# The up product of an MLP by seven products of halves, with its result sent through DRAM and the down product behind it

## The chip, the core and the metric

The kernel runs on one core of a Trainium2 chip. The time is that of one execution on the device, in microseconds. Of the core's engines five matter: TensorE (PE, with its weight loads as PEld), VectorE (DVE), ScalarE (ACT), GpSimd (POOL) and SyncE (SP), which here only issues DMAs. Each works off its own instructions in a fixed order and waits for the others by semaphores.

## What is computed

One decoder layer for 512 tokens of width 2048: an RMSNorm, three kinds of mixing heads, an output projection with residual, a second RMSNorm, and an MLP with the square of a ReLU; at the end one more RMSNorm. All is float32. The change is in the last third:

```python
    x = x + y @ w_out
    h2 = rmsnorm(x, norm2_w)
    return x + jnp.square(jax.nn.relu(h2 @ w_up)) @ w_down
...
    return rmsnorm(x, final_norm_w)
```

`w_up` is 2048 x 8192, `w_down` 8192 x 2048.

## The kernel before

**Numbers in halves.** Every float32 factor is split into a high part of type float32r (a cast on ScalarE) and a low part (the source minus the high part, on VectorE). `mm3` (lines 106 to 110) then makes a product of three matmuls: high by high, high by low, low by high. A weight tile that comes in by DMA costs one cast and one subtraction (`wload`, lines 96 to 104, for 128 x 512; `split`, lines 806 to 808, for 128 x 1024).

**Output projection** (lines 738 to 758). For each of 16 blocks m of 128 features 48 matmuls of 512 columns give the new x, feature by row. ScalarE and VectorE split it, scaled by the norm's weight, into `xw2[m]`; POOL adds up its squares; `turn` transposes it for the residual `xq`, which stays in SBUF token by row.

**Up product** (`up_chunk`, lines 765 to 777). For each of 64 blocks f of 128 hidden features four weight chunks of 256 KB are loaded and split, and 48 matmuls with `xw2` as the 512 moving columns give h. VectorE applies ReLU and the norm's factor `Rb`, ScalarE squares into `hp`.

**Down product** (`unit`, lines 881 to 912). Blocks of four f are multiplied with 1024 x 512 weights by seven products of halves in place of eight (Strassen's way in Winograd's form): h is cut in two by tokens and by features, the weights by features and by outputs. `a_prep` makes the seven left sides, four of them sums of h, `w_prep` the seven right sides from four quarters of 512 KB (`quarter`), four of them by a subtraction in place on VectorE or two. Each of the seven units has 12 matmuls of 512 columns, and VectorE adds its result to one or two of the four parts of `xq` (line 877).

**Order.** Up and down stand interleaved: `up_chunk` for block b + 1 before each unit of block b, so that a unit is followed by 12 matmuls that don't depend on it. The last block of four is multiplied plainly (`last`, line 944) and followed by the final norm. A scheduler places the other engines' instructions; weight loads have a raised priority (`DPRIO`, `APRIO`). All DMAs are issued by SP. PSUM tiles and SBUF pools are cyclic: a tile waits until the one that had its place is read.

Of the kernel before, what the change touches and what calls it, by code (L numbers as in the profile page):

```python
# [11 lines left out]
F32 = mybir.dt.float32  # L12
# [4 lines left out]
P = 128  # L17
# [11 lines left out]
FBLK = 4  # L29
ORDER = [10, 11, 12, 6, 7, 8, 9, 0, 1, 2, 3, 13, 4, 14, 5, 15]  # L30
# [23 lines left out]
def trunk(ctx, tc, xT, wv1, wv2, wa, wo, wu, wd, vec, wf, out, dbg=None):  # L54
# [655 lines left out]
    ps_l = psum_pool("ps_l", r=1, t=2)  # L710
# [7 lines left out]
    late = ctx.enter_context(tc.tile_pool(name="late", bufs=1, reuse_waits="tile"))  # L718

    xq = [[[late.tile([P, 2, 512], F32, name=f"xq{h}{d}{j}") for j in range(2)] for d in range(2)] for h in range(2)]  # L720

    def xw2t(shape, name, dt):
        return late.tile(shape, dt, name=name, tag="xw2", bufs=16, align_bytes=256)

    x1, xw2 = [], []
    acc2 = big_pool.tile([P, 512], F32, name="acc2", tag="acc")

    def turn(m):

        d, j = divmod(m // 4, 2)  # L730
        for q in range(m % 4, m % 4 + 2):
            p = xps("t")
            for b in range(NB):
                PE.transpose(p[:, b * P:(b + 1) * P], x1[m - m % 4 + q][:, b * P:(b + 1) * P], ident)  # L734
            for h in range(2):
                S.copy(out=xq[h][d][j][:, :, q * P:(q + 1) * P],
                       in_=p[:, h * 256:h * 256 + 256].rearrange("p (i f) -> p i f", i=2))

    for m in range(KT):
        xr = big_pool.tile([P, 512], F32, name="xr", tag="xr", bufs=6)  # L740
        nc.sync.dma_start(out=xr, in_=xT[:, m, :])
        p = gemm(wo[m], yh)
        x = big_pool.tile([P, 512], F32, name="x1", tag="xr", bufs=6)
        V.tensor_tensor(out=x, in0=p, in1=xr, op=ALU.add)
        a = xw2t([P, 2, 512], "xw2", F32R)
        w = col(C_N2 + m)
        S.activation(out=a[:, 0], in_=x, func=AF.Copy, scale=w)
        V.scalar_tensor_tensor(out=a[:, 1], in0=x, scalar=w, in1=a[:, 0].bitcast(F32),
                               op0=ALU.mult, op1=ALU.subtract)
        if m == 0:  # L750
            S.activation(out=acc2, in_=x, func=AF.Square)
        else:
            sq = tmp()
            S.activation(out=sq, in_=x, func=AF.Square)
            G.tensor_tensor(out=acc2, in0=acc2, in1=sq, op=ALU.add)
        x1.append(x)
        xw2.append(a)
        if m % 2 == 0 and m:
            turn(m - 2)

    nblk = FF // P // FBLK
    HK = FBLK // 2
    hp = {}

    def up_chunk(f, c, st):

        if c == 0:
            st["p"] = mmps()
        p = st["p"]
        gemm_chunk(p, wu[f], xw2, c)  # L770
        if c == KT // CHUNK_KT - 1:
            g = f // HK
            if f % HK == 0:
                hp[g] = late.tile([P, HK, 512], F32, name="hp", tag="hp", bufs=3)
            t = tmp()
            V.scalar_tensor_tensor(out=t, in0=p, scalar=0.0, in1=Rb, op0=ALU.max, op1=ALU.mult)
            S.activation(out=hp[g][:, f % HK], in_=t, func=AF.Square)


    ust = {}  # L780
    NCH = KT // CHUNK_KT
    Rb = per.tile([P, 512], F32, name="Rb")
    for n in range(FBLK * NCH):
        if n == 1:
            p = xps("r")
            PE.matmul(p, lhsT=ones, rhs=acc2, start=True, stop=True)
            rsqrt_exp(Rb, p, 1.0 / D, None)
        if n == 2:
            turn(KT - 2)
        up_chunk(n // NCH, n % NCH, ust)  # L790
    ps_l.__exit__(None, None, None)
# [3 lines left out]


    mlp = ctx.enter_context(tc.tile_pool(name="mlp", bufs=1, reuse_waits="tile", side="right"))
    psd = tc.tile_pool(name="ps_m", bufs=1, space=bass.MemoryType.PSUM, reuse_waits="tile")
    psd_pool = psd.__enter__()
    pool_of_mm[:] = [psd_pool, 2]  # L800
    PROD = (1, 2, 5, 6, 3, 7, 4)

    def pair(role):
        return psd_pool.tile([P, 2, 512], F32, name="pp", tag=f"pp{role}", bufs=1)
# [4 lines left out]

    AC = {}  # L810
    HT = T // 2

    def atile(n):
        return mlp.tile([P, 2, HK, HT], F32R, name=f"A{n}", tag=f"A{n}", bufs=1, align_bytes=256)

    def a_prep(b, n):

        h0, h1 = hp[2 * b], hp[2 * b + 1]
        A11, A21, A12, A22 = h0[:, :, :HT], h0[:, :, HT:], h1[:, :, :HT], h1[:, :, HT:]
        sub = lambda o, x, y: V.tensor_tensor(out=o, in0=x, in1=y, op=ALU.subtract)  # L820

        def sums(m):
            AC[b, "s", m] = t = mlp.tile([P, HK, HT], F32, name="s", tag="s", bufs=2)
            return t

        with tc.high_priority(APRIO):
            if n == 5:
                V.tensor_tensor(out=sums(5), in0=A21, in1=A22, op=ALU.add)
            elif n == 6:
                sub(sums(6), AC[b, "s", 5], A11)  # L830
            elif n == 3:
                sub(sums(3), A12, AC[b, "s", 6])
            elif n == 7:
                sub(sums(7), A11, A21)
            AC[b, n] = o = atile(n)
            split(o, {1: A11, 2: A12, 4: A22}[n] if n in (1, 2, 4) else AC[b, "s", n])

    def quarter(b, j, kh, d):
        q = mlp.tile([P, HK, 512], F32, name="q", tag="q", bufs=5)
        nc.sync.dma_start(out=q, in_=wd[b, j, kh, d])  # L840
        return q

    def w_tile():
        return mlp.tile([P, 2, HK, 512], F32R, name="W", tag="W", bufs=3, align_bytes=256)

    def w_prep(b, j, n, st):

        with tc.high_priority(DPRIO):
            sub = lambda o, x, y: V.tensor_tensor(out=o, in0=x, in1=y, op=ALU.subtract)
            if n == 1:  # L850
                st["11"] = quarter(b, j, 0, 0)
                st["21"] = quarter(b, j, 1, 0)
                st["12"] = quarter(b, j, 0, 1)
                src = st["11"]
            elif n == 2:
                st["22"] = quarter(b, j, 1, 1)
                src = st["21"]
            elif n == 5:
                sub(st["11"], st["12"], st["11"])
                sub(st["12"], st["22"], st["12"])  # L860
                src = st["11"]
            elif n == 6:
                sub(st["11"], st["22"], st["11"])
                src = st["11"]
            elif n == 3:
                src = st["22"]
            elif n == 7:
                src = st["12"]
            else:
                sub(st["21"], st["21"], st["11"])  # L870
                src = st["21"]
            o = w_tile()
            split(o, src)
        return o
# [156 lines left out]
```

## Time and profile before

| | |
|---|---|
| median of three runs | 2233.23 us (2233.19 to 2234.73) |
| the profiled execution | 2231.28 us |
| its span in the profile | 2229.5 us |
| mean granted TensorE clock | 0.997 |
| matmuls recorded | 10394 |
| DMA traffic | 227.07 MB, mean 102 GB/s |

A page of the profile gives each engine's busy time and its share of the span, then the chain of work that ended last. Groups of instructions read: line, engine, operation, output tile <- input tiles, shape, count, then the busy time of the group, the mean of one in ns, and the idle time of the engine just before them with what ended it. Matmuls overlap each other in a pipe, so their pace is seen from the starts of two that follow each other, not from their durations. Windows give the busy time and the number of instructions of each engine in a stretch of the span.

### The profile page before, as it was taken

The page shows a single profiled execution, that of the slowest core. Times are in us where ns is not written, and L with a number is a line of the kernel's source. Part 1 is how long each engine was busy: PE and PEld are TensorE (multiplying, and loading weights), DVE is VectorE, ACT ScalarE, POOL GpSimd, SP SyncE. Part 2 cuts the span into 40 slices and gives each one's busy share as a digit, 9 for nine tenths or more (in the row PEclk, how much of TensorE's full clock was granted, in tenths as well). Part 3 has the DMA queues.
Part 4 walks back from the last instruction along what each step waited for, and adds up shares of the span by engine and source line. Part 5 has one row for each costly group of instructions (what it writes and reads, how often), then busy time and mean ns, then how long its engine had stood idle before and what let it go on. Part 6 is the DMA issues. An engine that isn't in the chain of part 4 may idle for free.

```text
span 2229.5 us, 28060 instructions
## 1 busy us (share of the span) xinstructions
PE 2202.9 (99%) x10394; PEld 1829.7 (82%) x10394; DVE 1610.3 (72%) x2269; ACT 947.5 (42%) x1571; POOL 69.0 (3%) x111
## 2 busy tenths in 40 slices
PE   9999999999999999999999999999999999999998
PEld 8887787778988888888888888888888888888886
DVE  6689899844666533477777777878878878778774
ACT  5745565333445433433334333333333434333434
POOL 0000000000000011000000000000000000000003
PEclk9999999999999999999999999999999999999999
DMA  6332223233222344433333333333343333333332
GB/s 188 99 98 85 71 82 87 80 90 85 81 84 82 108 114 118 144 107 109 95 110 112 87 110 107 92 117 100 94 123 91 101 112 92 111 104 95 116 111 80
DMA packets 112506, 227.07 MB, mean 102 GB/s; under 512 B 18448, under 2 KB 20624, under 8 KB 112368
## 3 DMA queue, kind: packets, MB, share of 16 engines
q1 hardware_dynamic: 112368, 225.26, 34.2%
q8 instruction: 82, 1.34, 0.3%
q14 instruction: 56, 0.46, 0.1%
HBM read 218.53 MB, written 6.68 MB: 101 GB/s over the span
## 4 chain that ended last, share of the span: by engine, by line
PE 90%; DVE 6%; DMA 1%; issue 1%; ACT 1%; SPq 0%; ACTq 0%; DVEq 0%
PE mm L108 19%; PE mm L109 19%; PE mm L110 19%; PE pp L110 9%; PE pp L109 9%; PE pp L108 9%; DVE wlo L103 1%; DVE Yq L437 1%; DVE tq L435 1%; PE mm L273 1%; PE mm L271 1%; PE mm L272 1%; DVE cv L341 1%; DMA raw<-in_wa_dram 0%; PE t L734 0%
## 5 line engine op out<-in xcount | busy, mean ns | idle before, releaser
L102 ACT CAST whi<-raw 128x512 fp32r<-128x512 f32 (+1 forms) x544 | 333.2, 613 | 613.8 <-PE mm L109 556.2
L103 DVE TENSOR_TENSOR wlo<-raw,whi 128x512 fp32r<-128x512 f32 (+1 forms) x544 | 371.4, 684 | 240.0 <-ACT whi L102 227.9
L877 DVE TENSOR_TENSOR xq<-pp,xq 128x1024 f32<-128x1024 f32 x240 | 290.8, 1222 | 203.1 <-PE pp L110 200.6
L108 PE MATMUL mm<-big,whi 128*128 128x512 f32 x1024 | 404.2, 395 | 2.2 <-DVE tmp L556 1.6
L110 PE MATMUL mm<-big,wlo 128*128 128x512 f32 x1024 | 403.3, 394 | 0.0
L109 PE MATMUL mm<-big,whi 128*128 128x512 f32 x1024 | 403.1, 394 | 0.0
L108 PE MATMUL mm<-xw,whi 128*128 128x512 f32 x1024 | 398.8, 389 | 0.0
L110 PE MATMUL mm<-xw,wlo 128*128 128x512 f32 x1024 | 398.4, 389 | 0.0
L109 PE MATMUL mm<-xw,whi 128*128 128x512 f32 x1024 | 398.3, 389 | 0.0
L807 ACT CAST W<-q 128x1024 fp32r<-128x1024 f32 x210 | 220.8, 1051 | 401.4 <-PE pp L110 398.7
L108 PE MATMUL pp<-W,A 128*128 128x512 f32 x840 | 326.8, 389 | 0.0
L109 PE MATMUL pp<-W,A 128*128 128x512 f32 x840 | 326.8, 389 | 0.0
L110 PE MATMUL pp<-W,A 128*128 128x512 f32 x840 | 326.8, 389 | 0.0
L808 DVE TENSOR_TENSOR W<-q,W 128x1024 fp32r<-128x1024 f32 x210 | 255.5, 1217 | 1.7 <-ACT W L807 1.7
L108 PEld LDWEIGHTS mm<-big,whi 128*128 128x128 f32 x1024 | 192.6, 188 | 41.2 <-DVE tmp L556 1.8
L109 PEld LDWEIGHTS mm<-xw,whi 128*128 128x128 f32 x1024 | 192.4, 188 | 40.2 <-issue 0.2
L110 PEld LDWEIGHTS mm<-big,wlo 128*128 128x128 f32 x1024 | 192.6, 188 | 39.7 <-DVE wlo L103 0.6
L108 PEld LDWEIGHTS mm<-xw,whi 128*128 128x128 f32 x1024 | 192.1, 188 | 40.1 <-issue 0.2
L110 PEld LDWEIGHTS mm<-xw,wlo 128*128 128x128 f32 x1024 | 192.0, 188 | 39.8
L109 PEld LDWEIGHTS mm<-big,whi 128*128 128x128 f32 x1024 | 192.7, 188 | 38.7 <-DVE big L715 0.3
L110 PEld LDWEIGHTS pp<-W,A 128*128 128x128 f32 x840 | 157.8, 188 | 32.9
L108 PEld LDWEIGHTS pp<-W,A 128*128 128x128 f32 x840 | 157.7, 188 | 32.7
(263 smaller groups left out, 2099.2 us busy)
## 6 DMA issues: line engine op xcount, KB each, us to landing
raw<-in_wu_dram SPq DMA_DIRECT2D x256, 256.0 KB
q<-in_wd_dram SPq DMA_DIRECT2D x128, 512.0 KB
raw<-in_wa_dram SPq DMA_DIRECT2D x192, 256.0 KB
raw<-in_wo_dram SPq DMA_DIRECT2D x64, 256.0 KB
xr<-in_xT_dram SPq DMA_DIRECT2D x32, 256.0 KB
raw<-in_wv_dram SPq DMA_DIRECT2D x16, 256.0 KB
out_dram<-xq SPq DMA_DIRECT2D x16, 256.0 KB
raw<-in_wv_dram SPq DMA_DIRECT2D x16, 134.0 KB
```

The source lines that it names most:

```text
L102: S.copy(out=hi[:, :n], in_=raw[:, :n])
L103: V.tensor_tensor(out=lo[:, :n], in0=raw[:, :n], in1=hi[:, :n].bitcast(F32), op=ALU.subtract)
L108: PE.matmul(p, lhsT=lh, rhs=rh, start=first, stop=False, skip_group_check=more)
L109: PE.matmul(p, lhsT=lh, rhs=rl, start=False, stop=False, skip_group_check=more)
L110: PE.matmul(p, lhsT=ll, rhs=rh, start=False, stop=last, skip_group_check=more)
L271: PE.matmul(o, lhsT=xw[k][:, 0, s], rhs=hi[:, ws], start=k == 0 and b % 2 == 0, stop=False)
L272: PE.matmul(o, lhsT=xw[k][:, 0, s], rhs=lo[:, ws], start=False, stop=False)
L273: PE.matmul(o, lhsT=xw[k][:, 1, s], rhs=hi[:, ws], start=False, stop=k == KT - 1 and b % 2 == 1)
L341: V.scalar_tensor_tensor(out=cv, in0=xp[:, i:i + 512], scalar=w(i), in1=cv, op0=ALU.mult, op1=ALU.add)
L807: S.copy(out=o[:, 0], in_=src)
L808: V.tensor_tensor(out=o[:, 1], in0=src, in1=o[:, 0].bitcast(F32), op=ALU.subtract)
L877: V.tensor_tensor(out=x, in0=p, in1=x, op=ALU.add)
```

## The change

The up product is now done by seven products of halves too, for two blocks f at a time (`up_pair`, 32 of them). The left sides are weights: a pair's 2048 x 256 weights lie in DRAM as four quarters of 128 x 1024 (by parity of the input block and by f); the right sides are halves of x by tokens and by parity of the input block, and their sums, which are made and split during the output projection (`XP`, `XS`, and x22 through DRAM). A product has 8 x 3 matmuls of 256 columns.

The weight sums are made differently, for up and down alike (`w_prep`): three quarters t, v and u are loaded by SP; t grows by the fourth quarter through a DMA that accumulates (issued by POOL, for product 5), by u on VectorE (6) and by v on VectorE (4); u grows by the fourth quarter through a second accumulating DMA (7). The order of products is 1, 2, 5, 6, 3, 4, 7. Signs move to the sums of x and of h.

Each pair's h and its four sums go to DRAM in one store of 1 MB (`hs`). After all of up the down product runs alone, in 8 blocks of eight f (the last one with four, and four by the plain product): its left sides are read back from `hs` and split (`a_prep`), each unit has 24 matmuls with two weight tiles, and the residual is read back from DRAM (`xs`).

```diff
-    PROD = (1, 2, 5, 6, 3, 7, 4)
+    PROD = (1, 2, 5, 6, 3, 4, 7)
...
+    def w_prep(n, st, src):
+
+        with tc.high_priority(DPRIO):
+            more = lambda t, kh, d: nc.gpsimd.dma_start(out=t, in_=src(kh, d), accum_op=ALU.add)
+            more_on_v = lambda t, u: V.tensor_tensor(out=t, in0=t, in1=u, op=ALU.add)
+            if n == 1:
+                st["t"] = quarter(src(0, 0))
+                st["v"] = quarter(src(1, 0))
+                st["u"] = quarter(src(1, 1))
+            elif n == 5:
+                more(st["t"], 0, 1)
+            elif n == 6:
+                more_on_v(st["t"], st["u"])
+            elif n == 4:
+                more_on_v(st["t"], st["v"])
+            elif n == 7:
+                more(st["u"], 0, 1)
+            o = mlp.tile([P, 2, 1024], F32R, name="W", tag="W", bufs=3, align_bytes=256)
+            split(o, st[{2: "v", 3: "u", 7: "u"}.get(n, "t")])
+        return o
...
+    def up_pair(g):
...
+        def mms(n, lo, hi):
+            p = banks[n]
+            for i in range(lo, hi):
+                xh, xl = x_side(n, i)
+                s = slice(i * P, (i + 1) * P)
+                mm3(p, Ws[n][:, 0, s], Ws[n][:, 1, s], xh, xl, n in (1, 2, 4, 5) and i == 0, i == KP - 1,
+                    n in (6, 7, 3))
...
+        h = h_tile()
+        for f in range(2):
+            V.scalar_tensor_tensor(out=z[f], in0=z[f], scalar=0.0, in1=Rb, op0=(ALU.max, ALU.min)[f], op1=ALU.mult)
+            S.activation(out=h[:, 2 * f:2 * f + 2], in_=z[f].rearrange("p (i t) -> p i t", i=2), func=AF.Square)
+        sums(h[:, 4:8], h[:, 0], h[:, 2], h[:, 1], h[:, 3])
+        nc.sync.dma_start(out=hs[g // HK][:, :, g % HK], in_=h)
...
+    def a_prep(b, n, ns):
 
         with tc.high_priority(APRIO):
+            t = dp.tile([P, HK, HT], F32, name="ha", tag="ha", bufs=3)
+            o = dp.tile([P, 2, HK, HT], F32R, name=f"A{n}", tag=f"A{n}", bufs=1, align_bytes=256)
+            nc.sync.dma_start(out=t[:, :ns], in_=hs[b][:, HSLOT[n], :ns])
+            split(o[:, :, :ns], t[:, :ns])
+            AC[n] = o
...
-    for b in range(nblk - 1):
-        for n in range(FBLK * NCH):
-            up_chunk((b + 1) * FBLK + n // NCH, n % NCH, ust)
-            if n < 14:
-                if n % 7 == 0:
-                    dst = {}
-                unit(b, n // 7, PROD[n % 7], dst)
+    for b in range(ND):
+        for j in range(2):
+            dst = {}
+            for n in PROD:
+                unit(b, j, n, dst, HK if b < ND - 1 else HK // 2)
```

What this does to the order on three queues follows. First, VectorE in the middle of the MLP. Before, the low parts of up's weight chunks (`wlo`) stood between the units' splits (`W`), subtractions (`q`) and additions (`xq`):

```order
L808 TENSOR_TENSOR W_11698<-q_11656,W_11698 128x1024
L103 TENSOR_TENSOR wlo_11755<-raw_11752,whi_11754 128x512
L877 TENSOR_TENSOR xq100_7208<-pp_11619,xq100_7208 128x1024
L808 TENSOR_TENSOR W_11735<-q_11654,W_11735 128x1024
L849 TENSOR_TENSOR q_11654<-q_11696,q_11654 128x1024
L776 SCALAR_TENSOR_TENSOR tmp_11651<-mm_11514,Rb_8637 128x512
L103 TENSOR_TENSOR wlo_11790<-raw_11787,whi_11789 128x512
L849 TENSOR_TENSOR q_11656<-q_11656,q_11654 128x1024
```

Now a pair of up alone, from its split of product 5 to that of product 7. Here q_12653 is t, q_12657 u and q_12655 v; h_12641 holds the sums of the pair before; L897 takes a product out of PSUM:

```order
L825 TENSOR_TENSOR W_12719<-q_12653,W_12719 128x1024
L734 TENSOR_TENSOR h_12641<-h_12641 128x256 x2
L836 TENSOR_TENSOR q_12653<-q_12653,q_12657 128x1024
L738 SCALAR_TENSOR_TENSOR h_12641<-h_12641 128x256
L897 TENSOR_TENSOR raw_12651<-pu_12692,tmp_12687 128x256
L738 SCALAR_TENSOR_TENSOR h_12641<-h_12641 128x256
L825 TENSOR_TENSOR W_12750<-q_12653,W_12750 128x1024
L825 TENSOR_TENSOR W_12779<-q_12657,W_12779 128x1024
L836 TENSOR_TENSOR q_12653<-q_12653,q_12655 128x1024
L825 TENSOR_TENSOR W_12808<-q_12653,W_12808 128x1024
L897 TENSOR_TENSOR raw_12652<-pu_12722,tmp_12777 128x256
L825 TENSOR_TENSOR W_12839<-q_12657,W_12839 128x1024
```

The splits of products 6 and 3 (W_12750, W_12779) now stand behind the split of 5, which reads t after its accumulate, and the second accumulate, into u, can't start before W_12779 is done.

Second, SP's queue at the end of the output projection, with what each row waits for. `xr_8635` is the residual for the last block, the `q` are the first weight quarters of up:

```order
L770 DMA xr_8635<-in_xT_dram 128x512
L829 DMA q_8757<-in_wu_dram 128x1024 [waits DMAHW6_49,DMAHW7_49,DVE_49,Activation_49]
L829 DMA q_8759<-in_wu_dram 128x1024 [waits DMAHW0_49,PE_49]
L829 DMA q_8761<-in_wu_dram 128x1024 [waits DMAHW1_49,PE_49]
L794 DMA x22_7221<-tmp_8719 128x256 [waits DMAHW2_49,Activation_49]
L829 DMA q_9021<-in_wu_dram 128x1024 [waits DMAHW3_49,PE_49]
```

Before, up's chunks came through the small `raw` tiles that the output projection uses as well, and the loads ran on across this place; now the first load waits for VectorE, which reads `xr_8635` there, and all others stand behind it.

Third, VectorE in the second half of a block of the down product: `ha` are the sums of h for the next block, read back from DRAM.

```order
L825 TENSOR_TENSOR W_18126<-q_17922,W_18126 128x1024
L825 TENSOR_TENSOR A3_18323<-ha_18322,A3_18323 128x1024
L825 TENSOR_TENSOR W_18142<-q_17943,W_18142 128x1024
L963 TENSOR_TENSOR xq101_16565<-pp_18091,xq101_16565 128x1024
L825 TENSOR_TENSOR W_18171<-q_18165,W_18171 128x1024
L825 TENSOR_TENSOR A4_18359<-ha_18358,A4_18359 128x1024
L825 TENSOR_TENSOR W_18192<-q_18186,W_18192 128x1024
```

All seven splits of the next block's left sides (`A`) lie in this half; the first half has none.

More of the change, by code (lines that the diff above doesn't have):

```diff
@@ L717, in trunk @@
     yp.__exit__(None, None, None)
[L718 to L737, printed above, removed]
+    lp = tc.tile_pool(name="late", bufs=1, reuse_waits="tile")
@@ L754, in trunk @@
             S.activation(out=sq, in_=x, func=AF.Square)
-            G.tensor_tensor(out=acc2, in0=acc2, in1=sq, op=ALU.add)
+            G.tensor_tensor(out=Rb, in0=Rb, in1=sq, op=ALU.add)
         x1.append(x)
[L757 to L777, printed above, removed]
@@ L780, in trunk @@
-    ust = {}
-    NCH = KT // CHUNK_KT
-    Rb = per.tile([P, 512], F32, name="Rb")
-    for n in range(FBLK * NCH):
[L784 to L791, printed above, removed]
+        yw.append(y)
+        i = m // 2
+        half_split(XP[i][:, m % 2:m % 2 + 1], y[:, :HT].unsqueeze(1))
@@ L804, in pair @@
         return psd_pool.tile([P, 2, 512], F32, name="pp", tag=f"pp{role}", bufs=1)
-    def split(o, src):
-        S.copy(out=o[:, 0], in_=src)
-        V.tensor_tensor(out=o[:, 1], in0=src, in1=o[:, 0].bitcast(F32), op=ALU.subtract)
     AC = {}
[L811 to L824, printed above, removed]
-        with tc.high_priority(APRIO):
[L827 to L836, printed above, removed]
```

252 lines of the change are left out of this document (175 added, 77 removed).

## The prediction

> **What bounds the kernel now.** I read the page first: the share of each engine, the clock, then the chain that ended last.
>
> ```profile
> span 2229.5 us, 28060 instructions
> PE 2202.9 (99%) x10394; PEld 1829.7 (82%) x10394; DVE 1610.3 (72%) x2269; ACT 947.5 (42%) x1571; POOL 69.0 (3%) x111
> PE 90%; DVE 6%; DMA 1%; issue 1%; ACT 1%; SPq 0%; ACTq 0%; DVEq 0%
> ```
>
> PE is busy 99% of the span and makes up 90% of the chain. A busy PE is not yet a PE at its pace, so the MLP, where the change is, was looked at by windows and by PE's waits from 915 us (about where up and down run) to the end.
>
> ```profile
> core 0: us, PE busy (x) PEld busy (x) DVE busy (x) ACT busy (x) POOL busy (x), PEclk, DMA share, GB/s
> 1000.00:1400.00 400.00, 400.00 (x1766) 331.20 (x1766) 311.37 (x337) 151.20 (x200) 0.00 (x0) 1.00 0.35 105
> PE mm L108 <- DVE xq L951: 0.6, 1, 0.6
> ```
>
> 1766 matmuls of 512 columns in 400 us are 0.2265 us each, at granted clock 1.00, and PE waits 0.6 us in the whole MLP. So before the change the MLP costs the number of its matmuls times 0.2265 us. VectorE is at 311 of 400 us, POOL does nothing, the DMA engines are used to 35%. Only fewer or shorter matmuls can help, and whatever makes PE wait is a loss.
>
> **PE's own work.** The up product has 64 x 16 x 3 = 3072 matmuls of 512 columns (the trace has 1024 on each of the lines 108 to 110). The change makes of it 32 pairs x 7 products x 8 x 3 = 5376 matmuls, each of 256 columns with a weight load of its own. The trace has such a shape in the value projection, with a new load for each matmul as well:
>
> ```profile
> L108 PE MATMUL mm<-xw,whi 128*128 128x512 f32 x1024 | 398.8, 389 | 0.0
> L271 PE MATMUL mm<-whi,big 128*128 128x256 f32 x128 | 36.2, 283 | 0.0
> 555.55 0.28 PE L271 MATMUL mm<-whi,big 128*128 128x256 f32 x1
> ...
> 568.50 0.28 PE L271 MATMUL mm<-whi,big 128*128 128x256 f32 x1
> ```
>
> The durations (389, 283 ns) overlap, so the pace is read from starts: between the two rows of the timeline lie 108 matmuls without a gap, 12.95 / 108 = 0.1199 us. That is more than half of 0.2265, so seven eighths of the columns don't cost seven eighths of the time. Before: 3072 x 0.2265 = 695.8 us. After: 5376 x 0.1199 = 644.6 us. **Term 1: -51.2 us.** The down product keeps its 2520 + 192 matmuls of 512 columns, and the output projection and the transposes keep theirs.
>
> A rule to weigh against this: the Trainium skill (TensorE: Matmul & The Clock Gate, Back-to-back issue gap) gives N / 2.4 + 2.5 ns as the warm gap. By it 5376 matmuls of 256 columns would take 587 us and 3072 of 512 columns 663 us, 76 us less. The trace disagrees by 11 ns at both widths, and the sum goes by the trace.
>
> **What feeds it.** Before, a weight quarter was split into high and low part, or subtracted from another on VectorE, and the up product stood between the units of the down product as cover. Now the up product runs alone, a product lasts only 24 x 0.1199 = 2.88 us, a pair of row blocks 7 x 2.88 = 20.14 us. Durations that it needs, from groups of the same size:
>
> ```profile
> L807 ACT CAST W<-q 128x1024 fp32r<-128x1024 f32 x210 | 220.8, 1051 | 401.4 <-PE pp L110 398.7 <-DMA q<-in_wd_dram 1.6 <-DVE q L849 1.1
> L808 DVE TENSOR_TENSOR W<-q,W 128x1024 fp32r<-128x1024 f32 x210 | 255.5, 1217 | 1.7 <-ACT W L807 1.7
> L849 DVE TENSOR_TENSOR q<-q 128x1024 f32<-128x1024 f32 x120 | 146.6, 1222 | 2.0
> L877 DVE TENSOR_TENSOR xq<-pp,xq 128x1024 f32<-128x1024 f32 x240 | 290.8, 1222 | 203.1 <-PE pp L110 200.6
> L398 DVE TENSOR_TENSOR MT<-i,g 128x256 f32<-128x256 f32 x12 | 5.0, 417 | 1.5 <-PE i L396 1.4
> L776 DVE SCALAR_TENSOR_TENSOR tmp<-mm,Rb 128x512 f32<-128x512 f32 x64 | 44.1, 689 | 15.2 <-PE mm L110 14.0
> ```
>
> VectorE per pair: 7 splits and 2 additions at 1.22, 4 takes and 4 sums at 0.42, 2 at 0.69: 15.7 of 20.14 us. ScalarE has 7 casts at 1.05 and six smaller operations, 11 us at most. Work alone fits under PE. What need not fit is the order: two of the four weight sums are now DMAs that POOL issues and that add into a quarter in SBUF, and VectorE works off a fixed order. From the order above (the additions and splits of products 4 and 7 that follow there run while u is accumulated), one turn of the loop is: split of product 5, two sums, addition t+u, sum, take, sum, splits of 6 and 3; then the accumulate into u may start; cast and split of 7, split of the next pair's 1; then the accumulate into t may start; cast of 5, and round again. VectorE can't run ahead past a split whose quarter hasn't landed. In it stand 5 splits (6.09), 1 addition (1.22), 5 small operations (2.09), 2 casts (2.10), and six hand-offs between engines at 0.03 to 0.1 us (below, a cast begun at 919.27 ends at 920.32 and its split starts at 920.35), 0.3 in all: **11.8 us, plus twice the time D** from the end of a split to the accumulated quarter. PE's 20.14 us hide the loop while D is below (20.14 - 11.8) / 2 = **4.2 us**; beyond that each us of D costs 2 us a pair.
>
> No accumulating DMA is in the trace, nor any DMA issued by POOL's queue. The nearest rows, the first three from timelines, the last two from the chain in order of time:
>
> ```profile
> 914.62 2.54 SPq L840 DMA_DIRECT2D q<-in_wd_dram  x5
> 919.27 1.05 ACT L807 CAST W<-q 128x1024 fp32r<-128x1024 f32 x1 [1.38 <-DMA q<-in_wd_dram]
> 920.35 1.23 DVE L808 TENSOR_TENSOR W<-q,W 128x1024 fp32r<-128x1024 f32 x1 [1.73 <-ACT W L807]
> 399.48 3.20 DMA sm<-MT
> 403.80 2.14 DMA Bq<-sm
> sm<-MT SPq DMA_DIRECT2D x6, 256.0 KB
> Bq<-sm SPq DMA_DIRECT2D x24, 16.0 KB
> ```
>
> A plain load of 512 KB, first of five in a row, was used 4.65 us after its issue (914.62 to 919.27); 256 KB took 3.20 and 16 KB 2.14 us. Low end for D: 3.2, as if only half of the bytes counted. High end: 2.14 plus twice the 2.51 that the 512 KB added, 7.2, as the destination has to be read too. I take **4.9**, a little over the plain load that it is nearest to: the queue it runs beside carries three such loads and a store of 1 MB a pair. The loop is then 11.8 + 9.8 = 21.6 us, 1.46 over PE, in 31 pairs. **Term 2: +45 us** (ends 0 and 188). In the down product twelve matmuls (2.72 us) use one weight tile and four tiles lie between the split of 1 and that of 5, so D should stay hidden there.
>
> **The edges.** Up start: the first weight quarters lie in memory that the output projection and its last residual use, so their loads are issued only after it ends. One operation (0.69), a load (4.65), a cast (1.05) stand bare; then group 0 waits again for its first accumulate and for four tiles read back from DRAM behind eight loads. I take 14 us, ends 7 and 20. Down start: the sums of h are read into memory of the up product's right sides; a load and a cast less one product (2.88), and the next sums queue on SP behind eight residual tiles and the last store. Take 9, ends 3 and 13. Down: VectorE has, in the half block in which the next block's seven sums are split, 14 splits, 4 additions, 8 accumulations, 7 splits, 33 x 1.22 = 40.3 us, against 168 x 0.2265 = 38.05 of PE; in the other half 26 x 1.22 = 31.7. The three weight tiles of lead take most of the 2.2 us. Take 5 in all, ends 0 and 16. Tail: the last weights are split into memory of the sums, so they come later than now. Take 6, ends 0 and 10. **Term 3: +34 us**, ends 10 and 59. The output projection gains splits and sums of x on VectorE, 2 x 0.42, 4 x 0.42 and 1.22 = 3.7 us per two blocks that take PE 2 x 48 x 0.2265 = 21.7 us, and the xq additions fall from 240 to 128: both lie under PE and cost nothing now; without PE's cover the first would be 8 x 3.7 = 30 us.
>
> **Sum**, against the profiled execution's 2231.28 us (span 2229.5): -51.2 + 45 + 34 = +27.8, 2259.1. The median of the three runs, 2233.23, is 1.95 above that execution, so I say **2261 us**.
>
> **Rivals.** *The accumulates are hidden*: D below 4.2. PE then keeps its pace and the time is 2233.2 - 51.2 + 34 = 2216 us (2192 to 2241 with the ends of term 3), not slower. For it: 256 KB in 3.20 us, and a DMA share of 0.35. Against it: the 4.65 us. The decision lies at 4.2 us of D and nowhere else. The Trainium skill (DMA: Bandwidth & Descriptors, Anatomy of one DMA — SWDGE (gpsimd) path) fits a DMA issued by GpSimd by 2.0 us + bytes / 436e3, which makes an estimated 3.2 us for 512 KB and would give this rival; it speaks of plain copies, and no run here shows one.
>
> *The accumulates are long*, D of 6.5 because they read twice and share the DMA engines with the loads and stores of h: the loop is 24.8 us, 4.66 over PE, +144: 2360 us. For it: with the destination read and h written, traffic a pair is 3 x 0.5 + 2 x 1 + 1 = 4.5 MB in 20 us, some 225 GB/s, twice the 105 of now. Against it, the window of the kernel's start (columns as above):
>
> ```profile
> 0.00:56.00 56.00, 53.28 (x318) 47.50 (x319) 34.23 (x62) 33.40 (x65) 3.87 (x14) 1.00 0.61 189
> ```
>
> There 189 GB/s took 0.61 of the DMA engines, so 225 would take three quarters.
>
> *The matmuls aren't shorter*: if the weight load (188 ns as recorded) set the pace, 5376 of them would take over 1000 us. The 0.1199 us with a load each speaks against it so plainly that I give it nothing.
>
> **How the numbers follow.** Forecast (D 4.3 to 6) 0.43, with its own range 2225 to 2320; hidden 0.37; long 0.20. The range of all three is 2195 to 2360: it leaves out the best edges of the hidden case and the longest accumulates, some 0.17. About 0.2% is what a measurement of this kernel tells from no change. Faster: 0.32 of the hidden case and 0.03 of the forecast with short waits and edges, 0.35. Same: 0.03 + 0.04 = 0.07. Slower: 0.02 + 0.36 + 0.20 = 0.58.
>
> **What would show it.** Term 1: 256-column matmuls starting every 0.12 us inside a product. Term 2: in the up product, PE's waits before products 5 and 7 for ScalarE or VectorE, whose own idle time ends on the DMA into q; a pair lasting 21.6 us. At 20.2 us the hidden rival is right. Term 3: bare PE after the output projection and at the first block of down, and VectorE near 95% in down. Wrong altogether if VectorE's operations are longer beside POOL's DMAs, or if down waits for its accumulates too.

## The result, and the profile after

The changed kernel takes **2419.02 us** (median of four runs, 2417.65 to 2423.40) against 2233.36 us before: 1.083 times the time, 95% interval 1.081 to 1.085. The profiled execution has a span of 2415.9 us at a granted clock of 0.975. Forecast were 2261 us, at most 2360: the sign is right, the size is not.

First the page of the changed kernel: engines, the chain by engine, the two groups of splits, the accumulating DMAs with their median time from issue to landing.

```profile
span 2415.9 us, 33083 instructions
PE 2245.7 (93%) x12698; PEld 1942.2 (80%) x12698; DVE 1656.8 (69%) x2320; ACT 1045.8 (43%) x1630; POOL 177.4 (7%) x235
issue 55%; PE 34%; DVE 4%; POOL 2%; DMA 2%; ACT 1%; SPq 0%; POOLq 0%; ACTq 0%; DVEq 0%
L824 ACT CAST W<-q 128x1024 fp32r<-128x1024 f32 x434 | 443.3, 1048 | 846.0 <-DMA q<-in_wu_dram 356.0
L825 DVE TENSOR_TENSOR W<-q,W 128x1024 fp32r<-128x1024 f32 x434 | 520.6, 1222 | 341.3 <-ACT W L824 340.4
q<-in_wu_dram POOLq DMA_DIRECT2D x64, 512.0 KB, 7.2
q<-in_wd_dram POOLq DMA_DIRECT2D x60, 512.0 KB, 7.8
```

PE has fallen from 99% to 93% of the span and from 90% to 34% of the chain, where "issue" now has 55%. What that is shows in the chain in order of time (start, us, what): the stretches from one accumulating DMA to the next, for which the chain finds no releaser.

```profile
1231.51 13.59 issue
1245.10 0.04 POOLq L835
1245.14 0.83 POOL q L835
1245.98 11.82 issue
```

No engine took PE's place: VectorE is at 69%, its split still lasts 1222 ns. What grew is idle time, and the cast, first step of every split, points to where it comes from: 356 us in which ScalarE waited for a DMA into `q` in up. Three windows, one in up and two in down (columns as in the prediction):

```profile
1000.00:1400.00 400.00, 346.67 (x2635) 331.73 (x2635) 230.58 (x301) 142.82 (x204) 27.85 (x32) 0.96 0.55 144
1860.00:2100.00 240.00, 237.00 (x1033) 192.71 (x1032) 206.13 (x179) 108.10 (x106) 20.89 (x24) 1.00 0.68 183
2100.00:2340.00 240.00, 231.36 (x986) 185.62 (x984) 200.61 (x179) 101.42 (x103) 20.01 (x23) 0.99 0.61 160
```

In up 2635 matmuls take 400 us. A pair of row blocks has 168, so it lasts 400 x 168 / 2635 = 25.5 us where PE's work is 20. The waits of PE and ScalarE in up, and of ScalarE in down (us in total, times, longest):

```profile
PE pu L110 <- ACT W L824: 75.0, 73, 2.9
PE pu L112 <- DVE W L825: 36.2, 49, 0.8
```

These 111 us are not all that PE loses in up: its busy time grows too, 346.67 us for 2635 matmuls or 0.1316 us each, where the late kernel (below) has 0.1186.

```profile
ACT W L824 <- DMA q<-in_wu_dram: 356.0, 59, 8.0
ACT W L824 <- DVE q L836: 130.2, 62, 2.4
```

```profile
ACT W L824 <- DMA q<-in_wd_dram: 139.4, 45, 6.6
```

One turn of the loop, from the timelines of POOL and of ScalarE. The brackets say how long the engine sat idle and what ended it:

```profile
1193.57 0.86 POOL L835 DMA_DIRECT2D q<-in_wu_dram  x1 [12.92 <-DVE W L825]
1204.68 0.89 POOL L835 DMA_DIRECT2D q<-in_wu_dram  x1 [10.24 <-DVE W L825]
1220.05 0.88 POOL L835 DMA_DIRECT2D q<-in_wu_dram  x1 [14.49 <-DVE W L825]
```

```profile
1200.83 2.94 ACT L824 CAST W<-q 128x1024 fp32r<-128x1024 f32 x3 [5.12 <-DMA q<-in_wu_dram]
...
1212.01 1.04 ACT L824 CAST W<-q 128x1024 fp32r<-128x1024 f32 x1 [7.96 <-DMA q<-in_wu_dram]
```

The accumulate into u is issued at 1193.57 and the cast of product 7 begins at 1200.83; the one into t is issued at 1204.68 and the cast of product 5 begins at 1212.01. Each accumulate is issued when a VectorE split ends, and each of these casts begins when the accumulate has landed: the two waits stand in one line, and nothing else runs ahead.

### The profile page after: what moved, and what is told of

Same layout as the page of the kernel before. It is cut to its first block, busy times and chain, and to the rows that moved or that the text cites. A ratio compares the mean times of both kernels' runs of the same rounds, so it can differ in the third digit from the quotient of the medians.

```text
span 2415.9 us, 33083 instructions
## 1 busy us (share of the span) xinstructions
PE 2245.7 (93%) x12698; PEld 1942.2 (80%) x12698; DVE 1656.8 (69%) x2320; ACT 1045.8 (43%) x1630; POOL 177.4 (7%) x235
## 4 chain that ended last, share of the span: by engine, by line
issue 55%; PE 34%; DVE 4%; POOL 2%; DMA 2%; ACT 1%; SPq 0%; POOLq 0%; ACTq 0%; DVEq 0%
PE mm L110 9%; PE mm L111 9%; PE mm L112 9%; POOL q L835 2%; DVE Yq L439 1%; PE mm L275 1%; PE mm L273 1%; PE mm L274 1%; DVE wlo L105 1%; DVE tq L437 1%; DMA q<-in_wd_dram 1%; DMA tmp<-x 0%; PE v L200 0%; PE v L201 0%; DVE W L825 0%
## 5 line engine op out<-in xcount | busy, mean ns | idle before, releaser
L824 ACT CAST W<-q 128x1024 fp32r<-128x1024 f32 x434 | 443.3, 1048 | 846.0 <-DMA q<-in_wu_dram 356.0
L825 DVE TENSOR_TENSOR W<-q,W 128x1024 fp32r<-128x1024 f32 x434 | 520.6, 1222 | 341.3 <-ACT W L824 340.4
L110 PE MATMUL pu<-XS,W 128*128 128x256 f32 x1024 | 307.9, 301 | 62.6 <-ACT W L824 61.3
L110 PE MATMUL pp<-W,A 128*128 128x512 f32 x840 | 329.2, 395 | 16.3 <-ACT W L824 12.6
L112 PE MATMUL pu<-XS,W 128*128 128x256 f32 x1024 | 307.8, 301 | 36.2 <-DVE W L825 36.2
L111 PE MATMUL pp<-W,A 128*128 128x512 f32 x840 | 332.1, 395 | 5.0 <-DVE W L825 4.5
L112 PE MATMUL pp<-W,A 128*128 128x512 f32 x840 | 329.7, 393 | 1.0 <-DVE A L825 0.8
L111 PE MATMUL pu<-XS,W 128*128 128x256 f32 x1024 | 300.0, 293 | 0.0
L105 DVE TENSOR_TENSOR wlo<-raw,whi 128x512 fp32r<-128x512 f32 (+1 forms) x288 | 193.9, 675 | 147.0 <-ACT whi L104 133.3
L104 ACT CAST whi<-raw 128x512 fp32r<-128x512 f32 (+1 forms) x288 | 174.1, 606 | 267.0 <-PE mm L111 227.1
L110 PEld LDWEIGHTS pu<-XS,W 128*128 128x128 f32 x1024 | 205.7, 201 | 77.0 <-ACT W L824 76.4
L112 PEld LDWEIGHTS pu<-XS,W 128*128 128x128 f32 x1024 | 206.5, 202 | 46.7 <-DVE W L825 46.2
L111 PEld LDWEIGHTS pu<-XS,W 128*128 128x128 f32 x1024 | 205.7, 201 | 0.0
L110 PEld LDWEIGHTS pp<-W,A 128*128 128x128 f32 x840 | 159.1, 189 | 57.3 <-ACT W L824 20.5
L111 PEld LDWEIGHTS pp<-W,A 128*128 128x128 f32 x840 | 159.1, 189 | 46.5 <-DVE W L825 12.3
L112 PEld LDWEIGHTS pp<-W,A 128*128 128x128 f32 x840 | 159.1, 189 | 34.2 <-DVE A L825 2.1
```

Of the source, the lines that this page charges most:

```text
L104: S.copy(out=hi[:, :n], in_=raw[:, :n])
L105: V.tensor_tensor(out=lo[:, :n], in0=raw[:, :n], in1=hi[:, :n].bitcast(F32), op=ALU.subtract)
L110: PE.matmul(p, lhsT=lh, rhs=rh, start=first, stop=False, skip_group_check=more)
L111: PE.matmul(p, lhsT=lh, rhs=rl, start=False, stop=False, skip_group_check=more)
L112: PE.matmul(p, lhsT=ll, rhs=rh, start=False, stop=last, skip_group_check=more)
L824: S.copy(out=o[:, 0], in_=src)
```

## The experiments

For the ratios of the later runs the kernel before was run beside them; its medians were 2230.6 to 2231.5 us there.

### Is it the accumulates, and is it their wait or their traffic?

`no_accumulate` drops both DMAs, `late_accumulate` issues each of them after the last split that reads its quarter:

```diff
             elif n == 5:
-                more(st["t"], 0, 1)
...
-            elif n == 7:
-                more(st["u"], 0, 1)
             o = mlp.tile([P, 2, 1024], F32R, name="W", tag="W", bufs=3, align_bytes=256)
             split(o, st[{2: "v", 3: "u", 7: "u"}.get(n, "t")])
+            if n == 4:
+                more(st["t"], 0, 1)
+            elif n == 7:
+                more(st["u"], 0, 1)
```

(The last four lines are in `late_accumulate` alone.)

> Leaves out a part of the computation: both accumulating DMAs, in up and in down, so products 5, 6, 4 and 7 run with sums that lack the fourth quarter. All matmuls, splits, additions on VectorE and loads by SP are as in the changed kernel. Chain theory (the loss is the in-order loop of 11.8 us plus twice the 7.2 us from issue to landing): without the accumulates a pair takes PE's 20.1 us instead of the 25.5 seen, 32 x 5.4 = 173 us less, and down loses its 12 us of waits as well: 2235 us, at most 2250; the granted clock in up goes back to 1.00, since PE no longer waits. Rival, form (256-column matmuls with a load each don't hold their pace or the clock in a long row): over 2350, and the clock stays at 0.96. Rival, edges (the starts and the tail cost the time): 2419 less almost nothing. The traffic rival (the accumulates read and write SBUF and slow the other transfers) expects 2235 here as well.

> The same accumulating DMAs with the same bytes on the same queue, but each issued after the last split that reads its quarter, so that no split waits for it (the sums lack the fourth quarter, a part of the computation that is left out). Chain theory: as without accumulates, 2235 us, at most 2255, with the time from issue to landing still about 7.2 us. Traffic rival (the 1 MB a pair that is read, added and written back slows loads, VectorE or the weight tiles): near the changed kernel, over 2350, with PE's waits still on ScalarE behind q from SP.

Measured: 2198.01 us without them (ratio to before 0.986, 0.984 to 0.988), and **2203.64 us** with them out of every wait (0.988, 0.986 to 0.990). The rivals of form and of edges fall, and so does traffic: the same 65 MB on the same queue cost some 5.6 us when nobody waits for them, and the two intervals overlap. Both came out over 30 us faster than the 2235 I had expected, so more of the loss hangs on the waits than up's alone. The late kernel's window:

```profile
1000.00:1400.00 400.00, 400.00 (x3372) 400.00 (x3371) 295.51 (x382) 196.65 (x262) 34.83 (x40) 1.00 0.68 185
```

PE never waits there: 3372 matmuls in 400 us, 0.1186 us each, 19.9 us a pair, at clock 1.00 and with the DMA engines busier (0.68) than in the changed kernel (0.55).

### What the time to landing is made of

Four runs change only the accumulating DMA or what runs beside it: a plain copy on the same queue, half of its columns, the store of h issued after product 6 of the next pair, and no loads by SP in up after the first pair.

```diff
-            more = lambda t, kh, d: nc.gpsimd.dma_start(out=t, in_=src(kh, d), accum_op=ALU.add)
+            more = lambda t, kh, d: nc.gpsimd.dma_start(out=t, in_=src(kh, d))
```

```diff
+            more = lambda t, kh, d: nc.gpsimd.dma_start(out=t[:, :512], in_=src(kh, d)[:, :512], accum_op=ALU.add)
```

```diff
             take(n)
+            if n == 6:
+                store()
...
-        nc.sync.dma_start(out=hs[g // HK][:, :, g % HK], in_=h)
+        stores.append((g, h))
```

```diff
-                st["t"] = quarter(src(0, 0))
-                st["v"] = quarter(src(1, 0))
-                st["u"] = quarter(src(1, 1))
+                if not st:
+                    st["t"] = quarter(src(0, 0))
+                    st["v"] = quarter(src(1, 0))
+                    st["u"] = quarter(src(1, 1))
```

(In the last, `st` is one for all pairs of up.)

> The two DMAs stay where they are and on GpSimd's queue, but copy the fourth quarter over t and u in place of adding it (the sums are left out). The loop is the same, only the time D from issue to landing can change. If the adding makes D long (the destination read as well), D falls to that of a plain load, 3.2 to 4.7 us, the loop to 18.2 to 21.2 us, and the time to 2235 to 2270 us. If GpSimd's queue itself makes D long, D stays near 7.2 and the time near 2419. The Trainium skill (DMA: Bandwidth & Descriptors, Anatomy of one DMA — SWDGE (gpsimd) path) makes an estimated 3.2 us of a plain 512 KB copy on this queue.

> The accumulating DMAs add only the first 512 of the 1024 columns (half of each sum is left out), 256 KB in place of 512 KB; everything else and the order stay. Chain theory: D falls by about half of what is above the fixed part of 2.1 us, to 4.7 us, the loop to 21.2 us, 1.1 over PE, and the time to 2235 + 31 x 1.1 = 2270 us; in general the time has to be 2235 + 31 x (11.8 + 2 x D - 20.1) for the D that is measured. Traffic rival: half of the accumulated bytes, so half of the loss, about 2330 us, whatever D is.

> The store of h and its sums (1 MB) goes out after product 6 of the next pair in place of right after the sums, where the trace shows it 2.9 us ahead of the accumulate into u (1242.24 and 1245.12 us); nothing else is changed, the same bytes move. In the changed kernel the accumulate into t reaches its cast 5.6 to 6.6 us after its issue, the one into u, beside the store and three loads, 7.6 to 8.8. Contention theory (the store makes the second one long): the u accumulate falls to 5.6 to 6.5, the pair from 25.6 to about 23.5 us, the time from 2419 to about 2350. Rival, fixed latency (the accumulate takes what it takes, the store is no matter): within 10 us of 2419.

> In up only the first pair's quarters t, v and u are loaded by SP; all later pairs go on with the tiles as they stand (their weights are left out of the computation). Both accumulating DMAs, all splits and additions and their order stay. In the changed kernel the accumulate into t reaches its cast 6.2 us after its issue (mean of 20 between 1000 and 1500 us), the one into u, 0.8 us behind which SP issues three loads of 512 KB, 7.7 (mean of 17). Contention theory (those loads make the second one long): u falls to about 6.2, the pair to 11.8 + 12.4 = 24.2 us from 25.6, the time to some 2375 us. Rival, the second is long for another reason: the pair stays at 25.6 and the time within 15 us of 2419. If the first falls too, towards the 4 us that the plain copy had at best, the loads' traffic counts for both: 11.8 + 8 to 10 = 20 to 22 us, 2240 to 2300.

From the timelines between 1000 and 1500 us: the mean time from issue on POOL to the start of the cast that reads the quarter (19 to 23 of each kind), the mean pair, and what is left of it. The last four are single runs.

| run | time, us | t | u | pair | pair - t - u |
|---|---|---|---|---|---|
| changed kernel | 2419.0 | 5.93 | 7.75 | 25.57 | 11.89 |
| store_later | 2416.4 | 5.90 | 7.77 | 25.58 | 11.91 |
| no_loads_in_up | 2363.4 | 5.70 | 6.38 | 23.98 | 11.90 |
| plain_gpsimd_dma | 2291.5 | 4.62 | 5.77 | 22.31 | 11.92 |
| half_accumulate | 2286.8 | 4.18 | 5.97 | 22.36 | 12.21 |

The last column is the point: in five kernels the pair is 11.9 to 12.2 us plus the two times to landing, whatever these are. (The 6.2 us for t in the last expectation is 0.3 too long.) The store is no matter (2.6 us, about half of the range of the changed kernel's own runs). The loads by SP are: without them u falls by 1.4 us and t by 0.2, and the time to 2363 us, near the 2375 expected. Adding is the larger part: the plain copy is 1.3 us faster for t and 2.0 for u, and POOL issues it in 0.53 us in place of 0.87. Both expectations for the plain copy were off, 2291 between 2270 and 2419: it lands later than I had allowed for a plain load, 5.2 us in the mean with 3.86 as the fastest. Half the bytes still took 4.18 and 5.97 us, so the time is 2287 us and not 2270; the traffic rival's 2330 is further off. With the measured mean of 5.1 us the formula of that expectation gives 2292.

### Taking the latency out of the loop

`one_on_vector` and `both_on_vector` undo one or both accumulates in up; down stays.

```diff
                 st["u"] = quarter(src(1, 1))
+                if on_v:
+                    st["f"] = quarter(src(0, 1))
+            elif n in on_v:
+                more_on_v(st["t" if n == 5 else "u"], st["f"])
...
+            Ws[n] = w_prep(n, st, lambda kh, d: wu[g, kh, d], (5, 7))
```

(`(7,)` for one.) `other_order` keeps both accumulates and interleaves the products of two pairs:

```diff
...
-    for g in range(FF // P // 2):
-        up_pair(g)
+    for g in range(NG2 + 1):
+        for n, back in ((1, 0), (4, 1), (2, 0), (7, 1), (5, 0), (6, 0), (3, 0)):
+            if 0 <= g - back < NG2:
+                product(g - back, n)
```

> In up alone the second accumulate (into u) is undone: the fourth quarter is loaded by SP with the others and added to u on VectorE, 1.22 us; the accumulate into t stays, and down keeps both. Chain theory: the loop has one D in place of two, 11.8 + 1.2 + 5.6 to 6.6 = 18.6 to 19.6 us, just under PE's 19.9 (168 x 0.1186), so up is nearly free of waits: 2204 (as with late accumulates) plus some 30 that down's own accumulates cost: 2235 us. Rival, halves (each accumulate costs what it costs, the sum is what counts): half of 215 us comes back, 2311.

> In up both accumulates are undone: four loads per pair by SP, four additions on VectorE; down keeps its accumulating DMAs. Chain theory: VectorE has 15.7 + 2.4 = 18.1 us of work in a pair of 19.9 us of PE, no latency stands in its order: up as with late accumulates, and down's accumulates still there, 2204 + 30 = 2234 us, 2225 to 2245. Rival, VectorE as the bound (91% in a fixed order leaves PE waiting before products whose sums queue behind others): over 2270, with PE's waits in up on VectorE's splits and no wait on a DMA into q.

> Both accumulating DMAs stay, in up the products of two pairs are interleaved: 1 of the next pair, 4 of this one, 2 of the next, 7 of this one, 5, 6, 3 of the next; so three splits stand between each accumulate's start and the split that reads it. Down is unchanged. Chain theory: the loop holds one D (from the split of 3 by the accumulate into u to the split of 7, then 5, 6 and 3): 7 or 8 + 2.3 + 4 x 1.22 + 1.2 and small operations, some 17 us, under PE's 19.9, so the accumulates cost nothing in up although they take as long: 2204 + 30 = 2234 us, 2225 to 2250. Rival, accumulates are dear as such (their traffic, GpSimd's queue): over 2350. Rival, new waits (two pairs share PSUM banks and the four temporary tiles): 2260 to 2300, with PE's waits in up on ScalarE's or VectorE's takes.

Measured: 2279.9 (a single run), 2231.55 (ratio 1.000, 0.999 to 1.001) and 2250.1 us (1.009, 1.007 to 1.012). With both additions on VectorE up runs without waits, though VectorE now works 343 of 400 us (first row); it is no bound there. With the other order up is as fast (second row), and its accumulates cost nothing there, although each still takes 5.9 us to land (median):

```profile
1000.00:1400.00 400.00, 400.00 (x3372) 400.00 (x3371) 342.68 (x422) 196.76 (x262) 0.00 (x0) 1.00 0.47 159
```

```profile
1000.00:1400.00 400.00, 400.00 (x3368) 400.00 (x3367) 295.22 (x381) 189.64 (x260) 34.81 (x40) 1.00 0.68 185
```

Its extra 18.5 us over `both_on_vector` lie elsewhere, the most of them in one place, PE's waits for left sides of down (15.3 us, one of them 13.0; 3.8 us in `both_on_vector`); what makes them late was not tried and stays open. Waits of PE from 920 to 2200 us:

```profile
PE pp L110 <- ACT A L824: 15.3, 3, 13.0
PE pp L110 <- ACT W L824: 11.8, 14, 2.2
```

`one_on_vector` missed by 45 us. The turn of the loop is seen on VectorE, from the end of the wait for t's accumulate to the split that releases the next:

```profile
1225.38 1.23 DVE L825 TENSOR_TENSOR W<-q,W 128x1024 fp32r<-128x1024 f32 x1 [1.70 <-ACT W L824]
...
1229.58 2.36 DVE L825 TENSOR_TENSOR W<-q,W 128x1024 fp32r<-128x1024 f32 x2 [0.16 <-ACT W L824]
1231.86 2.35 DVE L836 TENSOR_TENSOR q<-q 128x1024 f32<-128x1024 f32 x2
1234.25 2.44 DVE L825 TENSOR_TENSOR W<-q,W 128x1024 fp32r<-128x1024 f32 x2
...
1237.76 1.23 DVE L825 TENSOR_TENSOR W<-q,W 128x1024 fp32r<-128x1024 f32 x1 [0.71 <-ACT W L824]
```

The addition and the split of product 4, which ran while u was accumulated, now stand in line as well (half of the 2.35 and of the 2.44): 15.1 us from the cast at 1224.31 to the next issue at 1239.39, plus 5.5 to landing, 20.7 from issue to issue. This turn is a short one; the mean of 29 is 21.2 us, 1.3 over PE's 19.9, and 32 of these make 41 of the 48 us by which this run lies above `both_on_vector`. A hidden step that I took out of its cover came back at about its full price.

### Down

Of the 215 us between the changed and the late kernel, `both_on_vector` leaves 28: they are down's. Three runs on top of it, all with up's additions on VectorE:

- `down_first_half_vector`: the four additions on VectorE in the first half of each block of down, too (`(5, 7) if j == 0 else ()`).
- `early_accumulate`: in the second halves, besides, the accumulates go into tiles loaded a second time, ahead of need; `q` has nine tiles in place of eight.
- `skewed_down`: in place of these the units of two halves interleaved; `q` has nine tiles here too, and down a fourth pair of PSUM banks.

```diff
+                if early:
+                    st["t2"], st["u2"] = quarter(src(0, 0)), quarter(src(1, 1))
+                    more(st["t2"], 0, 1)
+                    more(st["u2"], 0, 1)
...
+            elif n == 5 and early:
+                st["t"] = st["t2"]
...
+            elif n == 7 and early:
+                st["u"] = st["u2"]
```

```diff
-    roles = [0, 1, 2]
...
-            st["p", n] = pair(roles[{1: 0, 2: 1, 5: 2, 4: 1}[n]])
+            st["p", n] = pair({1: 3 * j, 2: 1, 5: 2, 4: 2}[n])
...
-    for b in range(ND):
-        for j in range(2):
-            dst = {}
-            for n in PROD:
-                unit(b, j, n, dst, HK if b < ND - 1 else HK // 2)
+    sts = {}
+    for r in range(2 * ND + 1):
+        for n, back in ((1, 0), (4, 1), (2, 0), (7, 1), (5, 0), (6, 0), (3, 0)):
+            b, j = divmod(r - back, 2)
+            if 0 <= r - back < 2 * ND:
+                unit(b, j, n, sts.setdefault((b, j), {}), HK if b < ND - 1 else HK // 2)
```

> Both accumulates undone in up (four additions on VectorE), and in down in the first half of each block, where no left sides are split; the second halves keep the accumulating DMAs. Measured so far: 2231.6 with down's accumulates, 2203.6 with all accumulates taken out of every wait, so down's accumulates cost 28 us. Chain theory: half of that goes, as VectorE has 30 x 1.22 = 36.6 us of work in a first half of 38 us of PE: 2215 to 2222. Rival, VectorE as the bound of down (81.8 us with four more additions a block, over 76.1 of PE): nothing won or a loss, 2230 to 2250.

> As the run before, and in the second halves of down the accumulating DMAs go into quarters of their own (t and u are loaded a second time), so that they wait for those loads and for no split; q has nine tiles in place of eight. Chain theory: no split stands behind the time to landing unless the tiles come free too late; 2205 to 2215. Rival, transfers and tiles (five quarters where three were, in nine tiles, 1 MB more per two weight tiles): the loads come late, PE waits for ScalarE behind q from SP, 2225 to 2250.

> Up with four additions on VectorE, down with both accumulating DMAs but the units of two halves interleaved (1 of the next half, 4 of this one, 2 of the next, 7 of this one, 5, 6, 3), so that seven weight tiles stand between an accumulate's start and the split that reads it, in place of three; q has nine tiles, the quarters are loaded where they are first needed, and PSUM has a fourth pair of banks in down. Chain theory: seven tiles are 7 x 2.72 = 19 us, far over the 8 us to landing, so down runs as with late accumulates: 2203 us, 2196 to 2212, faster than before the change by over 1%. Rival, new waits (loads come later, the left sides of the next block are needed before the last products of this one): 2225 or more, with PE's waits on ScalarE's casts of W or A.

Measured: 2233.96 us (1.001, 1.000 to 1.002) for `down_first_half_vector`, so nothing won. That is the rival's time, and its reason, no room on VectorE, is half of the story. A window of late down; in one block the end of VectorE's longest idle stretch and of the next one; and PE in two stretches of 5 us (the one between them has 24 matmuls):

```profile
1860.00:2100.00 240.00, 234.09 (x1020) 190.51 (x1019) 218.65 (x192) 108.34 (x107) 10.46 (x12) 1.00 0.53 160
```

```profile
1882.63 1.23 DVE L825 TENSOR_TENSOR W<-q,W 128x1024 fp32r<-128x1024 f32 x1 [3.63 <-ACT W L824]
...
1919.60 1.22 DVE L825 TENSOR_TENSOR W<-q,W 128x1024 fp32r<-128x1024 f32 x1 [0.43 <-ACT W L824]
```

```profile
1880.00:1885.00 5.00, 4.56 (x19) 3.18 (x19) 2.37 (x3) 3.45 (x4) 0.00 (x0) 1.00 1.02 413
1890.00:1895.00 5.00, 3.50 (x15) 2.36 (x14) 5.00 (x5) 1.31 (x2) 0.00 (x0) 1.00 0.01 2
```

VectorE is busy 91% of the large window. In the half block that keeps its accumulates it sits idle for 3.6 us, behind a cast that waits for a DMA into `q`; then it works without a gap for 36.5 us, into the half with four more additions, and PE loses matmuls in both places. By its place in the order that DMA is the second accumulate into u (issued at 1871.47, cast at 1881.55). So the loss starts at an accumulate, and the additions take the room in which VectorE could have caught up. Without that wait the room nearly suffices: `early_accumulate`, with the same additions, came out at 2214.1 us in a single run, inside the 2205 to 2215 expected, with VectorE busier (93%):

```profile
1860.00:2100.00 240.00, 237.14 (x1042) 194.86 (x1041) 224.14 (x199) 110.74 (x109) 10.45 (x12) 1.00 0.63 195
```

And **2204.98 us for `skewed_down`, 0.988 times the time before (0.986 to 0.990)**: 1.2% below the kernel before and well below the changed one, with up's additions on VectorE and down's accumulates kept. Its window of late down:

```profile
1860.00:2100.00 240.00, 240.00 (x1061) 198.72 (x1060) 214.03 (x188) 111.84 (x111) 20.90 (x24) 1.00 0.66 185
```

1061 matmuls in 240 us are 0.2262 each, PE's full pace, with all of down's accumulates in place and VectorE at 89%. What the ninth tile and the fourth pair of banks do without the new order was not tried.

## Why the prediction was wrong, point by point

- **Term 1** (-51.2 us) holds and was a little short: in a stretch without waits a 256-column matmul takes 400 / 3372 = 0.1186 us, not 0.1199, which makes -58. The formula that the prediction weighs here, from the Trainium skill (TensorE: Matmul & The Clock Gate, Back-to-back issue gap), is there the gap of an isolated matmul; for a stream of weight loads and matmuls, as in this kernel, the page says that both set the spacing. So the 76 us were no rival of the sum, and nothing in it hung on them.
- **Term 2** is the step that failed. The formula, 11.8 us plus twice D, stood up in five kernels: counted from the issue the rest is 11.9 to 12.2, and 11.1 in the changed kernel once the 0.4 us from a split's end to each issue, which I had put into D, are taken out. What was wrong is its **D: I took 4.9 us, after the plain load, and from the issue alone it is 5.9 for t and 7.75 for u**, 7.2 in the mean with the 0.4. The pair is 25.6 us in place of 21.6, PE's 19.9 are exceeded by 5.6 us: 32 x 5.6 = 180 us, where I had +45; up is 178 us longer than in the late kernel (below). The high end of 7.2, with +188, was in the text and was nearly the truth; I cut it off by choosing 6.5 for the rival of long accumulates, and with it the range. That the high end hit is in part luck: it was 4.65 us for a plain load and 2.51 for reading the destination, and the runs show 5.6 for the plain copy (5.2 and the 0.4) and 1.6 for adding.
- Why D is long: adding costs 1.3 to 2.0 us over the plain copy, the loads beside it 0.2 and 1.4. The second is what I had argued away by the mean share of the DMA engines. That share is 0.68 with no wait in the late kernel and 0.40 with waits without loads (row below); an average says nothing of the 7 us in which three loads stand beside one accumulate. By the Trainium skill's fit (DMA: Bandwidth & Descriptors, Anatomy of one DMA — SWDGE (gpsimd) path) a plain copy has an estimated 3.2 us; the fastest here took 3.86 from issue to use and the means are 4.6 and 5.8, so the hidden rival had no ground even for a copy that doesn't add. The window of up in `no_loads_in_up`:

```profile
1000.00:1400.00 400.00, 359.48 (x2801) 341.07 (x2800) 243.97 (x317) 153.19 (x217) 29.59 (x34) 1.00 0.40 89
```

- **Down was called hidden and costs 28 us.** I counted four weight tiles between the split of product 1 and that of 5. There are three: with two tiles a unit, the second of 1 and both of 2. Four tiles of 2.72 us lie from split to split, 10.9, and cast and split of 5 take 2.3 of it: 8.6 us are left for the 0.4 us to the issue and the 7.8 to landing (median), nothing to spare, and ScalarE waited 139 us for DMAs into `q` there. With seven tiles (`skewed_down`) the time is within 1.3 us of the late kernel's.
- **Term 3**, the edges, +34: the late kernel's time is 27.6 us under the span of before, so with -58 of term 1 the edges are +30 by difference: right in size, though the four parts were not measured one by one. VectorE near 95% in down was not seen; it is 86% with waits and 89% without. I had reckoned 1.22 us for each of its operations, and 188 of them cover 214.03 us of the last window above, 1.14 each, since their durations overlap too.
- By phases, from the first matmuls of up and of down to the last of down (the first kind of each three, first and last start), the changed kernel and the late one:

```profile
L110 PE MATMUL pu<-XP,W x512: 274/282/582, 918.7 to 1722.8; 128*128 128x256 f32 x171
```

```profile
L110 PE MATMUL pp<-W,A x840: 387/389/795, 1748.4 to 2355.8; 128*128 128x512 f32 x168
```

```profile
L110 PE MATMUL pu<-XP,W x512: 279/281/582, 913.6 to 1542.2; 128*128 128x256 f32 x171
```

```profile
L110 PE MATMUL pp<-W,A x840: 387/389/796, 1564.9 to 2140.9; 128*128 128x512 f32 x168
```

Up starts 5.1 us later and lasts 829.7 against 651.3 us, down 607.4 against 576.0, the tail 60.1 against 61.0: 5.1 + 178.4 + 31.4 - 0.9 = 214.0, the whole of 2415.9 - 2201.9.

## What to carry to other kernels

A step that is taken off a busy engine and given to a DMA becomes a latency, and in a fixed order a latency is paid in full unless enough work of the same engines stands between its start and its reader. Write the loop down as operations plus latencies, and where the sum decides at a single number that no trace shows, keep the whole range of that number. Then change the order before the means: the same accumulating DMAs cost 215 us with one split between in up and three in down. With three in up (`other_order`) PE ran there without waits, and with seven in down (`skewed_down`) it did there; no run has both.

## What the runs showed of the hardware

- **An accumulating DMA into SBUF** of 512 KB takes 5.7 and 6.4 us (means for t and u) from issue to use with no loads by SP beside it and 5.9 and 7.75 with them; half of it takes 4.2 and 6.0 us with them, so it isn't in proportion to bytes. GpSimd needs 0.87 us to issue one and 0.53 for a plain copy.
- **The granted clock falls with the waits**: 0.96 in the window of up with pairs of 25.6 us, 1.00 with pairs of 22.3 to 24.0. It had no price of its own that these runs show, as the rest of the loop is 11.9 us at both.
- **VectorE stands still beside GpSimd's addition.** The subtraction of 128 x 256 into `XP` takes 0.41 us alone, and 1.4 to 1.5 in the 13 of 16 cases that begin while POOL adds up the squares:

```profile
772.58 0.41 DVE L731 TENSOR_TENSOR XP<-tmp,XP 128x256 fp32r<-128x256 f32 x1
780.93 1.50 DVE L731 TENSOR_TENSOR XP<-tmp,XP 128x256 fp32r<-128x256 f32 x1
```

```profile
780.76 1.40 POOL L784 TENSOR_TENSOR Rb<-Rb,tmp 128x512 f32<-128x512 f32 x1 [8.72 <-ACT tmp L783]
```

POOL's addition runs from 780.76 to 782.16 and VectorE's ends at 782.43, some 0.27 us behind it. The Trainium skill (SBUF — State Buffer, Who interferes with whom) says that a VectorE instruction with two inputs in SBUF contends with a GpSimd instruction that reads SBUF; this trace agrees, with 1.1 us lost here. PE shows no wait in the output projection, so its matmuls hid it.
